# A hybrid decoder layer on one core: the MLP's two matrix products by seven block products for eight

## The chip, the core and the metric

The kernel runs on 1 core of a Trainium2 chip. The time is device microseconds of one launch: the median of 3 runs before the change is 2604.46 us (2600.12 to 2609.98). Engines are named as in the profile: PE (TensorE's matmuls), PEld (its weight loads), DVE (VectorE), ACT (ScalarE), POOL (GpSimd), SP (SyncE, which here only issues DMAs).

## The reference

One inference step of one decoder layer, for 512 prompt tokens and 8 short sequences of 4 tokens, 544 tokens in all, with a model width of 2048 and an MLP width of 8192, in float32:

```python
h = rmsnorm(x, norm_mix_w)
x = x + concat(conv_group(h), delta_group(h)) @ w_out
x = x + square(relu(rmsnorm(x, norm_ffn_w) @ w_up)) @ w_down
y = rmsnorm(x, final_norm_w)
```

Beside y it returns the new states of the convolution and delta groups. The change touches the second and the third line; the lines on the two head groups stay as they are.

## The kernel before

Activations lie transposed, channels on the 128 partitions and tokens along the free axis, in two token halves of 272 (256 prompt and 16 sample tokens). A matmul takes a 128x128 piece of a weight tile and 272 tokens of an activation tile into a PSUM bank.

Every product in float32 is made of three in float32r: `product` (lines 133 to 138) multiplies w_hi by x_hi, w_hi by x_lo and w_lo by x_hi, where hi is the value rounded and lo is the rest. A weight tile comes by one DMA into one of two w_raw buffers, ACT copies it into one of three w_hi buffers (line 112), and DVE subtracts that from w_raw into one of three w_lo buffers (line 115); `ahead` has two more tiles in work than the one that PE uses. These steps have a higher priority than the rest of the program, from which a scheduler makes one fixed order per engine; each engine and each DMA queue then runs its own in turn and waits on semaphores.

The stages, in time:

- The mixer (input projection, convolution, delta rule), to about 850 us. The change leaves it as it is.
- The output projection: 16 output tiles over the first 12 of 16 contraction tiles (w_o1, 32 loads of 128x768), then over the last 4 (w_o2, 8 loads of 128x1024, 48 matmuls each). A sum of 544 tokens goes from PSUM onto the residual x2 on DVE (line 876, `add`). Under w_o2, x2 times the norm's weight is split into h2's x_hi and x_lo (lines 127 and 130), ACT squares x2 (line 899), and POOL sums the squares in ssq (line 903). The token factor r2 = 1 / sqrt(mean + eps) isn't in h2: it is taken into the relu later.
- The MLP in 8 chunks of 1024 hidden channels. Up: 16 loads of 48 matmuls; for each of 8 hidden tiles DVE makes max(ps, 0) * r2 into f_tmp (line 920), ACT squares it (921) and copies u_hi (924), DVE makes u_lo (925). Down: 16 loads of 48 matmuls, each followed by `add` (876). u of a chunk and x2 stay in SBUF.
- The last chunk's down by token halves, 32 loads of 24 matmuls, with squares (ACT, line 949) summed on POOL (951 and 953) and the final norm of the first half, rstd (`rstd_rows`, lines 140 to 153) and DVE's scaling (line 939), under the products of the second. The second half's norm and its stores end the program.

Of the kernel before, what the change touches and what calls it, by code (L numbers as in the profile page):

```python
# [50 lines left out]
def trunk(ctx, tc, a):  # L51
# [119 lines left out]
    with ExitStack() as mix:  # L171
# [268 lines left out]
        def b_slab(ps, i):  # L440
            """Gate, then the group's RMSNorm as a side task."""
# [38 lines left out]
        # ---- gated delta rule of two heads  # L480
        def delta(gi, kq, vT, og):
# [8 lines left out]
            # keys with tokens on partitions, their norms, and the scalars that follow from them  # L490
# [21 lines left out]
            # decayed Gram matrices: at[m, 0, c] the system, at[m, 1, c] the output weights  # L512
# [19 lines left out]
            # inverse of the unit triangular systems: 32 x 32 blocks by substitution  # L532
# [36 lines left out]
            # values with tokens on partitions  # L569
# [11 lines left out]
            # blocks of 64, then of 128  # L581
# [39 lines left out]
            # the scan over chunks  # L621
# [40 lines left out]
            # RMSNorm over the value channels, and the gate  # L662
# [23 lines left out]
        def delta_sample(gi, kqs, vsT, og):  # L686
            """The 8 short sequences of two heads; rows are (k, q of head 0, k, q of head 1)."""
# [66 lines left out]
            # S += k y^T of each sequence in one pass: the float32r parts stacked along the contraction  # L754
# [38 lines left out]
        # ---- the input projection, with the other work threaded between its products  # L793
# [74 lines left out]
    ssq = tile_in(fp, "ssq2", [P, 2, HT])  # L868
    r2 = tile_in(fp, "r2", [P, 2, HT])

    def f_tmp():
        return tile_in(fp, "f_tmp", [P, 2, HT], bufs=4)

    def add(ob, ps, h=slice(0, 2)):
        with urgent():
            V.tensor_tensor(x2[ob][:, h], x2[ob][:, h], ps, ADD)  # L876
# [213 lines left out]
```

## Time and profile before

| | |
|---|---|
| median of 3 runs | 2604.46 us (2600.12 to 2609.98) |
| span of the profiled execution | 2602.0 us |
| PE busy | 2567.2 us, 99% |
| DVE, ACT, POOL busy | 1187.2, 776.5, 303.4 us |
| output projection w_o2, by PE | from 995 to 1043.5 us |
| MLP but its last down chunk, by PE | from 1043.5 to 2487.3 us |
| last down chunk, by PE | from 2487.3 to 2587 us |
| HBM traffic over the span | 101 GB/s |

All times of stages are microseconds from the start of the profiled span. A page of the profile has busy time by engine, the span in slices, the chain of waits that ended last (followed back from the last instruction), and groups of like instructions; the trace behind it gives single instructions with start and length. A matmul's record is longer than the distance to the next one, since matmuls overlap; a stage's price of one is its length over their number.

### The profile page before, as it was taken

What the parts mean: (1) busy time and instruction counts of PE and PEld (TensorE: products, weight loads), DVE (VectorE), ACT (ScalarE), POOL (GpSimd) and SP (SyncE); (2) the same over time, 40 slices, a digit from 0 to 9 for tenths busy, and PEclk for the clock granted to TensorE, in tenths of its full rate; (3) what the DMA queues carried; (4) which work ended last, traced back from release to release, by engine and by line L of the source; (5) the groups of instructions that cost most, each with busy time, mean ns of one, the idle gap of its engine ahead of it and who ended that gap; (6) DMA issues with size and microseconds to landing.
All of it is one profiled execution on the core that took longest, in us unless ns stands there. A gap on an engine that the chain in (4) does not pass through costs nothing.

```text
span 2602.0 us, 47137 instructions
## 1 busy us (share of the span) xinstructions
PE 2567.2 (99%) x20453; PEld 2545.1 (98%) x20453; DVE 1187.2 (46%) x1919; ACT 776.5 (30%) x1107; POOL 303.4 (12%) x413
## 2 busy tenths in 40 slices
PE   8999999999999999999999999999999999999997
PEld 8999999999999999999999999999999999999997
DVE  8675575675576325333333333333333333333346
ACT  5425325324234214321221221221221221221243
POOL 4224124123214003000000000000000000000022
PEclk9999999998999999999999999999999999999999
DMA  6333333343334522222222222222233222222245
GB/s 190 94 99 128 92 102 118 87 117 103 90 102 128 187 89 90 90 90 88 85 89 90 89 83 89 90 90 83 88 90 90 89 83 89 90 89 83 89 146 175
DMA packets 99256, 264.76 MB, mean 102 GB/s; under 512 B 28228, under 2 KB 35048, under 8 KB 99048
## 3 DMA queue, kind: packets, MB, share of 16 engines
q1 hardware_dynamic: 94824, 252.16, 31.8%
q0 software_dynamic: 4224, 9.59, 1.1%
q8 instruction: 161, 2.64, 0.4%
q14 instruction: 47, 0.39, 0.1%
HBM read 246.59 MB, written 15.10 MB: 101 GB/s over the span
## 4 chain that ended last, share of the span: by engine, by line
PE 89%; DVE 6%; DMA 2%; ACT 1%; issue 1%; SPq 0%; POOL 0%; DVEq 0%; ACTq 0%
PE ps_big L138 83%; DVE w_lo L115 2%; PE ps_sm L138 2%; DMA w_raw<-in_w_down_dram 1%; DVE xm L553 1%; DVE tm L549 1%; DMA tn<-ti 1%; ACT w_hi L112 0%; DVE x L939 0%; PE ps_sm L524 0%; DMA ti<-xm 0%; PE ps_sm L730 0%; PE ps_sm L636 0%; PE ps_sm L270 0%; DVE x_lo L130 0%
## 5 line engine op out<-in xcount | busy, mean ns | idle before, releaser
L138 PE MATMUL ps_big<-x_hi,w_hi 128*128 128x272 f32 x4320 | 906.3, 290 | 1.2 <-ACT x_hi L127 0.9
L138 PE MATMUL ps_big<-x_lo,w_hi 128*128 128x272 f32 x4320 | 903.7, 290 | 1.1 <-DVE x_lo L124 0.8
L138 PE MATMUL ps_big<-x_hi,w_lo 128*128 128x272 f32 x4320 | 901.0, 289 | 2.6 <-DVE w_lo L115 2.6
L112 ACT ACTIVATE w_hi<-w_raw 128x1024 fp32r<-128x1024 f32 (+2 forms) x427 | 442.9, 1037 | 1515.3 <-PE ps_big L138 1414.9
L115 DVE TENSOR_TENSOR w_lo<-w_raw,w_hi 128x1024 fp32r<-128x1024 f32 (+2 forms) x427 | 540.7, 1266 | 420.9 <-ACT w_hi L112 393.0
L138 PEld LDWEIGHTS ps_big<-x_hi,w_hi 128*128 128x128 f32 x4320 | 682.1, 189 | 5.8 <-ACT x_hi L127 2.1
L138 PEld LDWEIGHTS ps_big<-x_hi,w_lo 128*128 128x128 f32 x4320 | 682.1, 189 | 3.9 <-DVE w_lo L115 3.3
L138 PEld LDWEIGHTS ps_big<-x_lo,w_hi 128*128 128x128 f32 x4320 | 678.9, 189 | 1.9 <-DVE x_lo L124 1.0
L138 PE MATMUL ps_big<-u_lo,w_hi 128*128 128x272 f32 x1792 | 373.0, 289 | 0.0
L138 PE MATMUL ps_big<-u_hi,w_lo 128*128 128x272 f32 x1792 | 370.9, 288 | 0.0
L138 PE MATMUL ps_big<-u_hi,w_hi 128*128 128x272 f32 x1792 | 370.8, 288 | 0.0
L876 DVE TENSOR_TENSOR x<-x,ps_big 128x544 f32<-128x544 f32 x144 | 103.9, 722 | 492.2 <-PE ps_big L138 492.2
L138 PEld LDWEIGHTS ps_big<-u_hi,w_lo 128*128 128x128 f32 x1792 | 281.8, 188 | 0.0
L138 PEld LDWEIGHTS ps_big<-u_hi,w_hi 128*128 128x128 f32 x1792 | 281.5, 188 | 0.0
L138 PEld LDWEIGHTS ps_big<-u_lo,w_hi 128*128 128x128 f32 x1792 | 280.8, 189 | 0.0
L951 POOL COPY ssq<-f_tmp 128x272 f32<-128x272 f32 x2 | 2.3, 1148 | 1461.9 <-ACT f_tmp L949 1461.9
L920 DVE SCALAR_TENSOR_TENSOR f_tmp<-ps_big,r 128x544 f32<-128x544 f32 x64 | 46.4, 725 | 252.0 <-PE ps_big L138 252.0
L138 PE MATMUL ps_sm<-u_hi,w_lo 128*128 128x272 f32 x256 | 73.8, 289 | 1.4 <-DVE w_lo L115 1.4
L138 PE MATMUL ps_sm<-u_hi,w_hi 128*128 128x272 f32 x256 | 73.6, 288 | 0.2 <-ACT w_hi L112 0.2
L138 PE MATMUL ps_sm<-u_lo,w_hi 128*128 128x272 f32 x256 | 73.6, 288 | 0.0
L387 DVE SCALAR_TENSOR_TENSOR tmp<-tmp,cw 128x568 f32<-128x568 f32 (+1 forms) x88 | 70.9, 809 | 2.7
L366 DVE TENSOR_TENSOR tmp<-ps_big,r 128x512 f32<-128x512 f32 x47 | 32.4, 688 | 74.8 <-PE ps_big L138 74.7
(297 smaller groups left out, 1620.5 us busy)
## 6 DMA issues: line engine op xcount, KB each, us to landing
w_raw<-in_w_down_dram SPq DMA_DIRECT2D x144, 512.0 KB, 3.5
w_raw<-in_w_up_dram SPq DMA_DIRECT2D x128, 512.0 KB, 3.5
w_raw<-in_w_in_dram SPq DMA_DIRECT2D x106, 512.0 KB, 3.6
w_raw<-in_w_o_dram SPq DMA_DIRECT2D x32, 384.0 KB, 3.2
s<-in_s_d_dram SPq DMA_DIRECT2D x16, 512.0 KB, 3.6
tmp<-cat SPq DMA_DIRECT2D x16, 272.0 KB, 4.1
x<-in_x_dram SPq DMA_DIRECT2D x8, 544.0 KB, 6.1
out_o_y_dram<-x SPq DMA_DIRECT2D x16, 272.0 KB, 2.5
```

Source lines behind the costliest of these rows:

```text
L112: S.activation(hi[:, c], raw[:, c], AF.Copy)
L115: V.tensor_tensor(lo[:, c], raw[:, c], hi[:, c].bitcast(F32), SUB)
L138: PE.matmul(ps[h], wp[:, c : c + P], xp[:, h, :], start=start and i == 0, stop=stop and i == 2)
L366: V.tensor_tensor(out_p.rearrange("p (a c) -> p a c", a=2), whole[:, :, :HP], r1[:, :, :HP], MUL)
L387: V.scalar_tensor_tensor(co[:, :n], buf[:, i : i + n], cw[:, wcol + i : wcol + i + 1], co[:, :n], MUL, ADD)
L549: V.tensor_tensor(t, xm[:, :, j : j + 1].broadcast_to([P, 8, n]), um[:, j : j + 1, j + 1 :].broadcast_to([P, 8, n]), MUL,)
L553: V.tensor_tensor(xm[:, :, j + 1 :], xm[:, :, j + 1 :], t, SUB)
L876: V.tensor_tensor(x2[ob][:, h], x2[ob][:, h], ps, ADD)
L920: V.scalar_tensor_tensor(t, ps[1], 0.0, r2, MAX, MUL)
L951: G.tensor_copy(ssq[:, h, :], sq[:, h, :])
```

## The change

w_up, w_down and the activations are seen as 2x2 blocks: a pair of output tiles, a pair of contraction tiles, and the two token halves. Seven products of combined blocks stand for eight, in Winograd's form of Strassen's algorithm. Each is made of three float32r matmuls a piece, as before.

- `Weights` loads four tiles (a11, a12, a21, a22; w_q, of the new pool g with 10 buffers) for a pair m. At product 6 DVE makes four combinations of them, three in place; for each of the seven products ACT copies w_hi and DVE makes w_lo.
- `combos_first` and `combos` make the activation's blocks: c0 (two blocks as they are), c1 and c2 (two combinations each) and c3 (one block), each as hi and lo. The four combinations go into a tile tc of the pool tt, which has two buffers and holds u, ui, ssq and rt as well. c0 and c1 lie in the 32 buffers hl, c2 and c3 in the 24 of the new pool cmb.
- `bilinear` runs the products in the order 1, 2, 6, 5, 7, 3, 4, pair by pair; the last two pairs of a sequence are interleaved. Up has 32 pairs of hidden tiles (8 contraction pairs, 24 matmuls a product). Down has 5 chunks of 6 contraction pairs, 8 pairs of output tiles each (18 matmuls a product); the last 4 of 64 contraction tiles are multiplied in the ordinary way by token halves (w_d2, 32 loads of 128x512).
- u of a pair is stored to DRAM (u_d) by POOL's queue, and loaded again by `prepare`, which combines it on POOL. A chunk's tiles are prepared during the chunk before it: the first after pair 1, the second after pair 3, the rest after pair 5. Residual sums x2 lie in DRAM (x2_d): a pair's tile is loaded, added to seven times, and stored.
- w_o2 goes by token halves (16 loads of 24 matmuls), and the whole norm, r2 included, is applied to x2 ahead of the split (`normalise`): the first half's under the products of the second, the second half's behind rstd_rows at the end, with `combos` on DVE.

The core of the diff:

```diff
+    cmb = pool("cmb", 24)
+    gp = pool("g", 10)
+    tt = pool("tt", 2)
+    sqp = pool("sq", 2)
...
+    x2_d = [tile_in(dram, f"x2d{i}", [P, 2, 2, HT]) for i in range(KT // 2)]
+    u_d = [tile_in(dram, f"ud{i}", [P, 2, 2, HT]) for i in range(FF // 256)]
...
+    def f32r_parts(pl, name, tag, src):
+        hi = tile_in(pl, name + "_hi", [P, 2, HT], F32R, tag=tag)
+        lo = tile_in(pl, name + "_lo", [P, 2, HT], F32R, tag=tag)
+        S.activation(hi, src, AF.Copy)
+        V.tensor_tensor(lo, src, hi.bitcast(F32), SUB)
+        return hi, lo
+    def combos_first(c, b11_b21):
+        hi, lo = f32r_parts(hlp, "c0", "hl", b11_b21)
+        c[1], c[2] = (hi[:, 0, :], lo[:, 0, :]), (hi[:, 1, :], lo[:, 1, :])
+    def combos(c, x, eng):
+        b11, b12, b21, b22 = (x[:, i, j, :] for i in range(2) for j in range(2))
+        t = t_tile("tc")
+        eng.tensor_tensor(t[:, 1, :], b12, b11, SUB)
+        eng.tensor_tensor(t[:, 0, :], b22, t[:, 1, :], SUB)
+        eng.tensor_tensor(t[:, 2, :], b22, b12, SUB)
+        eng.tensor_tensor(t[:, 3, :], b21, t[:, 0, :], SUB)
+        hi, lo = f32r_parts(hlp, "c1", "hl", t[:, 0:2, :])
+        c[6], c[5] = (hi[:, 0, :], lo[:, 0, :]), (hi[:, 1, :], lo[:, 1, :])
+        b = tile_in(cmb, "c3", [P, 2, HT], F32R, tag="c")
+        S.activation(b[:, 0, :], b22, AF.Copy)
+        V.tensor_tensor(b[:, 1, :], b22, b[:, 0, :].bitcast(F32), SUB)
+        c[3] = b[:, 0, :], b[:, 1, :]
+        hi, lo = f32r_parts(cmb, "c2", "c", t[:, 2:4, :])
+        c[7], c[4] = (hi[:, 0, :], lo[:, 0, :]), (hi[:, 1, :], lo[:, 1, :])
+    ORDER = (1, 2, 6, 5, 7, 3, 4)
...
+                    self.q = [g_tile("w_q", [P, self.n]) for _ in range(4)]
+                    for t, s in zip(self.q, self.src):
+                        nc.sync.dma_start(t, s)
...
+                if p == 6:
+                    self.s1 = tile_in(rawp, "w_s1", [P, 1024], tag="w_raw")[:, : self.n]
+                    V.tensor_tensor(self.s1, a21, a22, ADD)
+                    V.tensor_tensor(a21, a11, a21, SUB)
+                    V.tensor_tensor(a11, self.s1, a11, SUB)
+                    V.tensor_tensor(a12, a12, a11, SUB)
+                s = {1: a11, 2: a12, 6: a11, 5: getattr(self, "s1", None), 7: a21, 3: a12, 4: a22}[p]
+                hi = tile_in(whip, "w_hi", [P, 1024], F32R)[:, : self.n]
+                lo = tile_in(wlop, "w_lo", [P, 1024], F32R)[:, : self.n]
+                S.activation(hi, s, AF.Copy)
+                V.tensor_tensor(lo, s, hi.bitcast(F32), SUB)
+            return hi, lo
...
+            if p == 6:
+                at = flat.index(w)
+                for nxt in flat[at + 1 : at + 2]:
+                    nxt.load()
+            return w.parts(p)
...
+            ps = st[{2: "y", 5: "z", 3: "z"}.get(p, "x")]
+            c = cs(key)
+            for k, ck in enumerate(c):
+                xhi, xlo = ck[p]
+                for j, (wp, xp) in enumerate(((whi, xhi), (whi, xlo), (wlo, xhi))):
+                    PE.matmul(
+                        ps, wp[:, k * P : (k + 1) * P], xp,
+                        start=p in (1, 2, 5) and k == j == 0, stop=k == len(c) - 1 and j == 2,
+                        skip_group_check=True,
+                    )
+            st["out"](p, ps)
...
-    for oq, w in ahead(range(KT * N2 // 8), lambda q: weight(a["w_o2"][q], 1024)):
+    steps = [(h, q) for h in range(2) for q in range(KT * N2 // 8)]
+    for (h, oq), w in ahead(steps, lambda it: weight(a["w_o2"][it[1]], 1024)):
...
+        nc.gpsimd.dma_start(x2_d[oq][:, :, h, :], x2p[oq][:, :, h, :])
+        if h == 1:
+            if oq == 1:
+                rstd_rows(r2, [ssq], t_tile("rt", (P, 2, HT)), (0,))
+            if oq >= 2:
+                for i in {2: (0, 1), 7: (6, 7)}.get(oq, (oq - 1,)):
+                    normalise(i, 0)
+                    combos_first(h_c[i], x2p[i][:, :, 0, :])
+    with urgent():
+        rstd_rows(r2, [ssq], t_tile("rt", (P, 2, HT)), (1,))
+        for i in range(KT // 2):
+            normalise(i, 1)
+            combos(h_c[i], x2p[i], V)
...
+    def hidden(m):
+        t = t_tile("u").rearrange("p (a b) c -> p a b c", a=2)
+        def out(p, ps):
+            with urgent():
+                if p in (1, 6, 5, 4):
+                    d = {1: t[:, 0, 0], 6: t[:, 0, 1], 5: t[:, 1, 1], 4: t[:, 1, 0]}[p]
+                    S.activation(d, ps, AF.Copy)
+                else:
+                    add({2: t[:, 0, 0], 7: t[:, 1, 1], 3: t[:, 0, 1]}[p], ps)
+                if p in (3, 4):
+                    d = t[:, 0 if p == 3 else 1]
+                    V.scalar_tensor_tensor(d, d, 0.0, d, MAX, MUL)
+                    if p == 4:
+                        nc.gpsimd.dma_start(u_d[m], t)
...
+        return [[x] for x in w[:-2]] + [w[-2:]]
+    bilinear(pairs_of(NF, lambda m, q: a["w_up"][m, q], 1024), lambda m: h_c, hidden)
+    CH = 6
+    NCH = (NF - 2) // CH
+    u_c = {}
+    def load_u(k):
+        x = t_tile("ui").rearrange("p (a b) c -> p a b c", a=2)
+        nc.sync.dma_start(x, u_d[k])
+        return x
+    def prepare(k):
+        x, u_c[k] = load_u(k), [None] * 8
+        combos_first(u_c[k], x[:, :, 0, :])
+        combos(u_c[k], x, G)
+    def partial(key):
+        c, m = key
+        x = g_tile("x2v", [P, 2, 2, HT])
+        nc.sync.dma_start(x, x2_d[m])
+        def out(p, ps):
+            for b, h in {1: [(0, 0)], 2: [(0, 0)], 6: [(0, 1)], 5: [(1, 1)], 7: [(1, 1)], 3: [(0, 1)], 4: [(1, 0)]}[p]:
+                add(x[:, b, h], ps)
+            if p == 4:
+                nc.gpsimd.dma_start(x2_d[m], x)
+                if c + 1 < NCH and m in (1, 3):
+                    prepare(CH * (c + 1) + m // 2)
+                if c + 1 < NCH and m == KT // 2 - 3:
+                    for k in range(2, CH):
+                        prepare(CH * (c + 1) + k)
...
+    for k in range(CH):
+        prepare(k)
...
+    bilinear(groups, lambda key: [u_c[CH * key[0] + k] for k in range(CH)], partial)
+    u = []
+    for k in range(NCH * CH, NF):
+        x = load_u(k)
+        for b in range(2):
+            u.append(f32r_parts(hlp, "ul", "hl", x[:, b]))
...
-    for (h, ob), w in ahead(steps, lambda it: weight(a["w_down"][(NCH - 1) * KT + it[1]], 1024)):
+    for (h, ob), w in ahead(steps, lambda it: weight(a["w_d2"][it[1]], 512)):
```

Three places of the order that the scheduler makes of it. On DVE at the start of up, before: the last weight splits of the output projection, rstd (r_10067), and the first hidden tiles.

```order
L115 TENSOR_TENSOR w_lo<-w_raw,w_hi 128x1024
L150 TENSOR_TENSOR f_tmp<-r_10067 128x272 x2
L151 SCALAR_TENSOR_TENSOR f_tmp<-ps_sm,f_tmp 128x272 x2
L152 TENSOR_SCALAR f_tmp<-f_tmp 128x272 x2
L153 TENSOR_TENSOR r_10067<-r_10067,f_tmp 128x272 x2
L920 SCALAR_TENSOR_TENSOR f_tmp<-ps_big,r_10067 128x544
L115 TENSOR_TENSOR w_lo<-w_raw,w_hi 128x1024
L925 TENSOR_TENSOR u_lo<-f_tmp,u_hi 128x544
L115 TENSOR_TENSOR w_lo<-w_raw,w_hi 128x1024
```

The same engine and place now: the last step of rstd (r_88), the first pair's norm (L1008), its combinations tc (L920 to L923, now the lines of `combos`), splits of c3 (L928) and c2 (L909), and the next pair.

```order
L154 TENSOR_TENSOR r_88<-r_88,rt 128x272
L1008 SCALAR_TENSOR_TENSOR x_7_10063<-x_7_10063,nv,r_88 128x272
L1008 SCALAR_TENSOR_TENSOR x_0_10056<-x_0_10056,nv,r_88 128x272 x2
L920 TENSOR_TENSOR tc<-x_0_10056 128x272
L922 TENSOR_TENSOR tc<-x_0_10056 128x272
L921 TENSOR_TENSOR tc<-x_0_10056,tc 128x272
L928 TENSOR_TENSOR c_12226<-x_0_10056,c_12226 128x272
L923 TENSOR_TENSOR tc<-x_0_10056,tc 128x272
L1008 SCALAR_TENSOR_TENSOR x_1_10057<-x_1_10057,nv,r_88 128x272 x2
L909 TENSOR_TENSOR c_lo<-tc,c_hi 128x544
L920 TENSOR_TENSOR tc<-x_1_10057 128x272
```

Before, the splits of weights go on at once; now the norm and the combinations of the eight pairs stand between rstd and the sixth product's activations.

On SP at the change from up to down, now: the last loads for up, two quartets for down (the first of x2v and half a third quartet with them), and the loads of u for the first chunk.

```order
L946 DMA w_q<-in_w_up_dram 128x1024 x126
L946 DMA w_q<-in_w_d_dram 128x768 x8
L1084 DMA x2v<-x2d_10072 128x1088
L946 DMA w_q<-in_w_d_dram 128x768 x2
L1073 DMA ui<-ud_10080 128x1088
L1073 DMA ui<-ud_10081 128x1088
L1073 DMA ui<-ud_10082 128x1088
L1073 DMA ui<-ud_10083 128x1088
```

On POOL's queue beside it: the stores of the last two u tiles, then the combinations of the first u tile and the start of the second's.

```order
L1056 DMA ud_10110<-u 128x1088
L1056 DMA ud_10111<-u 128x1088
L920 TENSOR_TENSOR tc<-ui 128x272
L922 TENSOR_TENSOR tc<-ui 128x272
L921 TENSOR_TENSOR tc<-ui,tc 128x272
L923 TENSOR_TENSOR tc<-ui,tc 128x272
L920 TENSOR_TENSOR tc<-ui 128x272
```

Before, SP had only loads of w_raw there, and POOL had nothing between the second norm and the last chunk; now each load of ui and each tc follows the stores of u in its queue, and they share the two buffers of tt.

On DVE in down, before: a weight's split and a sum of 544 tokens for each 48 matmuls (an output tile).

```order
L876 TENSOR_TENSOR x_0_10050<-x_0_10050,ps_big 128x544
L115 TENSOR_TENSOR w_lo<-w_raw,w_hi 128x1024
L876 TENSOR_TENSOR x_1_10051<-x_1_10051,ps_big 128x544
L115 TENSOR_TENSOR w_lo<-w_raw,w_hi 128x1024
L876 TENSOR_TENSOR x_1_10051<-x_1_10051,ps_big 128x544
```

Now, the start of a pair m in the middle of a chunk: the weights' combinations (L953 to L956), splits (L961), and sums of 272 tokens onto x2v.

```order
L953 TENSOR_TENSOR w_s_21785<-w_q 128x768
L961 TENSOR_TENSOR w_lo<-w_q,w_hi 128x768
L954 TENSOR_TENSOR w_q<-w_q 128x768
L883 TENSOR_TENSOR x2v<-x2v,ps_s 128x272
L961 TENSOR_TENSOR w_lo<-w_q,w_hi 128x768
L955 TENSOR_TENSOR w_q<-w_s_21605,w_q 128x768
L883 TENSOR_TENSOR x2v<-x2v,ps_s 128x272
L956 TENSOR_TENSOR w_q<-w_q 128x768
L961 TENSOR_TENSOR w_lo<-w_q,w_hi 128x768
L883 TENSOR_TENSOR x2v<-x2v,ps_s 128x272
L961 TENSOR_TENSOR w_lo<-w_s_21605,w_hi 128x768
L883 TENSOR_TENSOR x2v<-x2v,ps_s 128x272
```

Each sum waits for the PE product it belongs to, and the weight work of the next products stands behind it in the same queue.

More of the change, by code (lines that the diff above doesn't have):

```diff
@@ L886, in trunk, with bank @@
         if q == 1:
-            add(ob, ps[1])
-    h2 = []
-    N2 = KT - N1
-    for oq, w in ahead(range(KT * N2 // 8), lambda q: weight(a["w_o2"][q], 1024)):
+            add(x2[ob], ps[1])
+    early.close()
+    small2 = pool("small2", 4, space=PSUM)
+    def bank(first):
+        t = tile_in(small2 if first else small, "ps_s", [P, 512], tag="sm2" if first else "sm")
+        return t[:, :HT]
+    def f32r_parts(pl, name, tag, src):
[4 more added lines that the diff above has]
+        return hi, lo
@@ new lines, in bilinear, with load @@
+    def bilinear(groups, cs, outs):
+        items = [(g, i, p) for g in range(len(groups)) for p in ORDER for i in range(len(groups[g]))]
+        flat = [w for g in groups for w, _ in g]
+        def load(it):
+            g, i, p = it
+            w = groups[g][i][0]
+            w.load()
+            if p == 6:
[3 more added lines that the diff above has]
+            return w.parts(p)
+        state = {}
+        for (g, i, p), (whi, wlo) in ahead(items, load):
+            w, key = groups[g][i]
+            if p == 1:
+                state[i] = {"x": bank(True), "out": outs(key)}
+            st = state[i]
+            if p in (2, 5):
+                st["y" if p == 2 else "z"] = bank(False)
+            ps = st[{2: "y", 5: "z", 3: "z"}.get(p, "x")]
[9 more added lines that the diff above has]
+            st["out"](p, ps)
@@ L894, in trunk @@
             for k in range(N2):
[L895 to L899 removed]
+                product({h: ps}, w, (N2 * j + k) * P, cat[N1 + k], k == 0, k == N2 - 1, (h,))
+            add(x2[ob][:, h], ps)
+            sq = tile_in(sqp, "sq", [P, HT])
+            S.activation(sq, x2[ob][:, h], AF.Square)
@@ new lines, in trunk @@
+    xt = [[None] * (KT // 2) for _ in range(2)]
+    def finish(h, pair):
+        t = xt[h][pair]
+        for j in range(2):
+            o = 2 * pair + j
+            V.scalar_tensor_tensor(t[:, j], t[:, j], nv[:, 32 + o : 33 + o], r3[:, h, :], MUL, MUL)
+        nc.sync.dma_start(a["o_y"][pair][:, :, h, :], t)
+    steps = [(h, o) for h in range(2) for o in range(KT)]
+    for (h, ob), w in ahead(steps, lambda it: weight(a["w_d2"][it[1]], 512)):
+        pair, j = divmod(ob, 2)
+        if j == 0:
+            xt[h][pair] = tile_in(cmb, "xt", [P, 2, HT], tag="c")
+            nc.sync.dma_start(xt[h][pair], x2_d[pair][:, :, h, :])
+        x = xt[h][pair][:, j]
+        ps = ps_small(HT)
+        for k in range(4):
+            product({h: ps}, w, k * P, u[k], k == 0, k == 3, (h,))
+        add(x, ps)
+        sq = tile_in(sqp, "sq", [P, HT])
+        S.activation(sq, x, AF.Square)
+        if ob == 0:
+            G.tensor_copy(ssq[:, h, :], sq)
+        else:
+            (G if ob < KT - 2 else V).tensor_tensor(ssq[:, h, :], ssq[:, h, :], sq, ADD)
```

112 lines of the change are left out of this document (48 added, 64 removed).

## The prediction

> **What bounds the kernel now.** I read the page first, then the busy time by stage, then the chain of waits, then single groups and DMA sizes. The first row is the page's line on TensorE.
>
> ```profile
> PE 2567.2 (99%) x20453; PEld 2545.1 (98%) x20453; DVE 1187.2 (46%) x1919; ACT 776.5 (30%) x1107; POOL 303.4 (12%) x413
> ```
>
> By stage (length, busy time of PE, PEld, DVE, ACT, POOL, granted clock, DMA share, GB/s): the second output projection, the MLP, its last down chunk, the end, and two stretches of the mixer.
>
> ```profile
> 980.00:1043.00 63.00, 63.00 (x500) 63.00 (x500) 39.62 (x45) 32.73 (x44) 24.24 (x16) 1.00 0.29 88
> 1043.00:2487.00 1444.00, 1444.00 (x11480) 1443.84 (x11479) 467.72 (x485) 334.74 (x369) 0.00 (x0) 1.00 0.29 88
> 2487.00:2587.00 100.00, 98.42 (x777) 97.13 (x775) 62.54 (x88) 44.67 (x65) 36.98 (x26) 1.00 0.57 170
> 2587.00:2602.00 15.00, 1.10 (x4) 0.30 (x2) 8.68 (x21) 1.35 (x3) 0.00 (x0) 0.61 0.43 149
> 700.00:750.00 50.00, 50.00 (x405) 49.85 (x403) 31.72 (x77) 17.57 (x50) 6.20 (x15) 1.00 0.31 91
> 750.00:800.00 50.00, 48.27 (x416) 46.75 (x415) 37.29 (x93) 10.49 (x12) 10.89 (x18) 0.95 0.37 107
> ```
>
> In the MLP PE never waits and every other engine is under a third busy: there a matmul less is its whole time less. The chain of waits (start, length) gives the price of one.
>
> ```profile
> 1044.43 1442.91 PE ps_big L138 x11472
> 2487.34 24.02 PE ps_sm L138 x191
> 2513.78 3.90 DMA w_raw<-in_w_down_dram
> ```
>
> 1442.91 / 11472 = 0.1258 us for each matmul. The last chunk, 32 loads for 24 matmuls each, takes 2487.3 to 2587, 3.12 us a load against 24 x 0.1258 = 3.02: two raw buffers only just feed it.
>
> **The change part by part.** The span is 2602.0 us, 2.5 below the median of 2604.46; I sum spans and add 2.5 at the end. Up to the last w_o1 tile nothing of weight moves.
>
> What it removes: the MLP had 8 x 32 x 48 = 12288 matmuls. Now up has 32 pairs x 7 products x 24 = 5376, the five down chunks 40 x 7 x 18 = 5040, the ordinary rest 32 x 12 = 384: 10800, so 1488 fewer, 187 us at 0.1258. Everything else is what this buys, and the question is how much of it PE then spends waiting.
>
> Prices on VectorE, from starts in its timeline (start, duration): what counts in a full queue is the distance of starts.
>
> ```profile
> 40.33 0.95 DVE L115 TENSOR_TENSOR w_lo<-w_raw,w_hi 128x768 fp32r<-128x768 f32 x1
> 41.19 0.72 DVE L239 TENSOR_TENSOR ssq<-ssq,tmp 128x544 f32<-128x544 f32 x1
> 41.83 0.41 DVE L253 TENSOR_TENSOR wst<-wab,wst 128x256 fp32r<-128x256 f32 x1
> 42.16 1.22 DVE L115 TENSOR_TENSOR w_lo<-w_raw,w_hi 128x1024 fp32r<-128x1024 f32 x1
> ```
>
> So 768 wide costs 0.86, 544 costs 0.64, 256 costs 0.33 (272: 0.35), and 1024 by the same slope 1.15. The end of the program, in the same view, prices the norm.
>
> ```profile
> 2586.93 0.44 DVE L876 TENSOR_TENSOR x<-x,ps_sm 128x272 f32<-128x272 f32 x1 [0.33 <-PE ps_sm L138]
> ...
> 2591.45 6.69 DVE L939 SCALAR_TENSOR_TENSOR x<-x,nv,r 128x272 f32<-128x272 f32 x16
> ```
>
> *w_o2 by halves.* 16 loads at 3.12 instead of 384 matmuls, 48.3 us: +1.7. Under its second half VectorE also gets the norm of the first and four-wide splits: per load 1.15 + 2 x 0.35 + 2 x 0.42 + 0.64 = 3.3 us, against 3.02, and more while POOL adds squares: early in the run, with POOL in a long add, the 768 split that takes 0.95 took twice that.
>
> ```profile
> 11.92 1.99 DVE L115 TENSOR_TENSOR w_lo<-w_raw,w_hi 128x768 fp32r<-128x768 f32 x1
> ```
>
> Six such loads: 2 to 8 us, I take 3. The MLP starts at 1043.5 + 4.7 = 1048.2. [...]
>
> *Start of up.* From the last add to the end of rstd was 4.5 us (2586.93 to 2591.45). Now there is a POOL add in it (1.4, below), three norm steps and one split between its VectorE steps (1.9) and some backlog: 9 us. Then product 6 of the first pair needs the combinations of all eight pairs, and VectorE's order has in front of the last one 16 norm steps (6.7), 32 combinations of 272 (11.2), 7 splits of 272 (2.5), 16 of 544 (10.2), 7 instructions of 1024 (8.1), one add, and about 1.5 us where one combination waits for another: 40.5 us. PE has 3 products to do in it, 72 x 0.1258 = 9.06. Wait: 9 + 40.5 + 0.5 - 9 = 41 us (36 to 46). Before, the MLP began without a gap, since its norm was put into f_tmp behind the products.
>
> *Up.* 5376 x 0.1258 = 676.3. Per pair VectorE has 11 x 1.15 + 3 x 0.35 + 2 x 0.75 = 15.2 us in 21.1, its bursts reach about 5.7 us at product 6 against two products of 3.02 of lead: covered, barely.
>
> *Up to down.* Sizes and landing times of DMAs, and POOL's groups (mean ns):
>
> ```profile
> x<-in_x_dram SPq DMA_DIRECT2D x8, 544.0 KB, 6.1
> out_o_y_dram<-x SPq DMA_DIRECT2D x16, 272.0 KB, 2.5
> out_o_ss_dram<-s POOLq DMA_DIRECT2D x8, 512.0 KB, 3.8
> w_raw<-in_w_o_dram SPq DMA_DIRECT2D x8, 512.0 KB, 3.5
> xr<-in_x_dram SPq DMA_DIRECT2D x7, 544.0 KB, 4.5
> ...
> cat<-tmp POOLq DMA_DIRECT2D x8, 256.0 KB, 2.8
> cat<-o_g POOLq DMA_DIRECT2D x8, 256.0 KB, 3.6
> ```
>
> ```profile
> L953 POOL TENSOR_TENSOR ssq<-ssq,f_tmp 128x272 f32<-128x272 f32 x24 | 34.7, 1445 | 43.5 <-ACT f_tmp L949 43.5
> ...
> L471 POOL DMA_DIRECT2D cat<-tmp x16 | 11.3, 735 | 37.3 <-DVE xm L553 32.9 <-DVE tmp L469 4.4
> ...
> L432 POOL TENSOR_TENSOR tmp<-tmp 128x512 f32<-128x512 f32 x8 | 10.3, 1283 | 23.6 <-DVE tmp L366 23.6
> ```
>
> The pool tt has two buffers, and both hold u of the last two pairs until their stores land. Then u is read back, one tile in one buffer and its combinations in the other, so the six preparations are serial: a load of 544 KB (4.5, bounds 3.5 and 6.1) and four POOL combinations (0.68 each by proportion from the 512-wide row, 1.45 by the 272 row; I take 0.9, since most of VectorE stands still then). Period 8.1 us. The first tile: last u but one done 3 us before the end, a copy and a square 1.2 us, 0.7 to issue, 3.8 to store, 4.5 to load: it lands about 8 us after up ends, the sixth at 8 + 5 x 8.1 = 48.5. Products 1, 2 and 6 need tile 6, so the wait is 48 us (38 at 3.5 and 0.68; 67 at 6.1 and 1.45).
>
> *Down.* 5040 x 0.1258 = 634.0. VectorE 11 x 0.86 + 7 x 0.35 = 11.9 us of 15.85 a pair, plus 2.3 for a preparation; weights, residual tiles and stores are 2.7 MB in 15.85 us, 170 GB/s, what the last chunk moves now, and the u tiles come on top. I put 6 us for small waits (0 to 30).
>
> *Four chunk boundaries.* 24 of 32 hl buffers and 18 of 24 cmb buffers are the running chunk's, so tiles 1 and 2 of the next are ready, the third is half written, and three of them are loaded and combined in series after it: tile 4 lands 1.5 us after the chunk's last product, tile 6 two periods later at 17.7: 17 us each, 68 together (48 to 100).
>
> *After a wait.* PE's clock falls when it idles: 0.95 over 50 us above, that is 5 us at half speed or 2.5 us lost, in a stretch with under 2 us of idling. At half clock two matmuls start 0.45 us apart, 0.225 each:
>
> ```profile
> 592.00:600.00 8.00, 8.00 (x56) 7.20 (x54) 4.97 (x18) 1.46 (x3) 1.03 (x1) 0.50 0.00 0
> ```
>
> ```profile
> 594.27 0.66 PE L138 MATMUL ps_big<-x_hi,w_hi 128*128 128x272 f32 x2
> 594.72 0.66 PE L138 MATMUL ps_big<-x_lo,w_hi 128*128 128x272 f32 x2
> ```
>
> Six waits at 2.5: 15 us. [...] But the row shows 8 us of work without a gap at half clock; what would follow from that is a rival below.
>
> *The rest.* ScalarE's copies of 850 to 1043 us by shape:
>
> ```profile
> L112 ACT ACTIVATE w_hi<-w_raw 128x768 fp32r<-128x768 f32 x28 | 23.7, 845 | 94.6 <-PE ps_big L138 94.6
> ...
> L112 ACT ACTIVATE w_hi<-w_raw 128x1024 fp32r<-128x1024 f32 x11 | 11.6, 1058 | 16.5 <-PE ps_big L138 14.9 <-ACT f_tmp L899 1.5
> ```
>
> 32 loads of 256 KB pass through two buffers, each held for the load (3.2, between 2.8 and 3.6), the copy (0.63 at 512 wide by these two) and VectorE's split (0.95 and 1.22 above give 0.68): 4.5 / 2 = 2.25 us a load, 72 us (64 to 80) for 48.3 of matmuls. The end, as now, 15 (2587 to 2602).
>
> Sum: 1048.2 + 41 + 676.3 + 48 + 640 + 68 + 15 + 72 + 15 = 2623.5, with 2.5 more 2626: 187 us are saved and some 209 given back, slower by 0.8%. A measurement of this kernel can tell about 0.5%, 13 us, from no change: 2591.4 to 2617.5 is the same.
>
> **The rivals.**
>
> *Short waits (faster).* The serial steps run at their lower bounds: loads of 3.5, combinations of 0.68. Then 1046 + 36 + 676.3 + 38 + 634 + 48 + 6 + 64 + 15 = 2563, 2566 as a median. For it: the 512 KB row, and that nothing else moves data while PE waits. Against: the two 544 KB rows, 4.5 and 6.1, and that c_hi and c_lo read the same tile while POOL does. A microsecond of the period is worth 5 + 4 x 2 = 13; with the small terms (after a wait, the rest, down's waits) at their lower ends too, 23 us, it decides from a period of 7.2 down: 23 + 0.9 x 13 = 35, which is 2591.
>
> *VectorE bounds down (slower still).* At product 6 four weight combinations and a split, 5 x 0.86 = 4.3 us and a ScalarE copy between, stand ahead of the PSUM adds; PE's lead is two products, 4.5 us. If each pair loses 1.5 us, 40 pairs lose 60: 2686. For it: 75% busy with adds that wait for PE in the same queue. Against: three weight buffers, and the order spreads the four over three products. It decides where VectorE passes 90% of a pair.
>
> *PE stays at half clock around every wait.* The last stage feeds PE 1.5 us of work in 2.25; at 0.225 a matmul a step is 2.7, 32 of them 86 instead of 72; and three products after each wait (6.8 us, up 9) at half speed cost 7 us instead of 2.5, six times 27: 2626 + 14 + 27 = 2667. For it: the row at 592. Against: 2487 to 2587 shows 1.00 with PE at 98%. [...]
>
> **How the numbers follow.** The forecast gets 0.42, with its own range from 2600 to 2655; short waits 0.30, VectorE 0.13, half clock 0.15. Faster by over 0.5%: short waits and a little of the forecast's lower end, 0.32. The same: 0.20, from the forecast. Slower: 0.48. The range runs from the first rival's 2566 to 2690, past the second's; half of short waits and part of VectorE lie outside.
>
> **What would show it.** PE's idle time before its first products: some 41 us near 1050 behind VectorE's splits, 48 near 1770 behind ui loads and POOL, four of 17 some 127 us of matmuls apart, each behind ui. Matmuls in up and down at 0.126. If the boundaries show under 12 us, or the ui period under 7.2, the first rival holds; if PE waits in every pair of down for VectorE, the second; if the granted clock after 2500 is under 0.8, the third. If PE's count isn't 1488 lower or its pace differs, all of it is wrong.

## The result and the profile after

The changed kernel takes 2650.55 us (median of 4 runs, 2645.77 to 2654.69) where the kernel before takes 2607.22 (4 runs, 2600.12 to 2611.01): a ratio of 1.0172, 95% interval 1.0148 to 1.0196. It is slower, as forecast, and inside the range, but by 1.7% instead of 0.8%: the loss is twice the one that the prediction worked out. The profiled execution has a span of 2652.8 us, against a predicted sum of 2623.5: 29 us are to be explained.

The page's line of busy time first. PE runs 1492 matmuls fewer (1488 by count; some records are missing) and 128 us less; VectorE has 673 us more to do, POOL 167.

```profile
PE 2439.2 (92%) x18961; PEld 2389.9 (90%) x18961; DVE 1860.5 (70%) x2899; ACT 1028.7 (39%) x1542; POOL 470.9 (18%) x639
```

By stage, as in the prediction (length, busy time of PE, PEld, DVE, ACT, POOL, granted clock, DMA share, GB/s): the start of up, up, the change to down with most of chunk 0's first products, the boundary to chunk 1, the steady part of chunk 1, and the w_d2 stage.

```profile
1041.00:1099.00 58.00, 25.88 (x101) 19.93 (x99) 55.12 (x107) 26.51 (x44) 5.80 (x7) 0.62 0.30 102
1099.00:1758.00 659.00, 658.28 (x5269) 658.28 (x5270) 496.96 (x505) 269.29 (x347) 15.99 (x30) 1.00 0.37 125
1758.00:1850.00 92.00, 48.66 (x301) 44.27 (x299) 54.56 (x75) 31.70 (x50) 37.07 (x40) 0.70 0.36 119
...
1942.00:2006.00 64.00, 42.77 (x293) 39.97 (x293) 48.57 (x63) 24.04 (x37) 28.85 (x27) 0.81 0.45 154
2006.00:2096.00 90.00, 90.00 (x721) 90.00 (x721) 73.96 (x107) 35.43 (x44) 2.97 (x6) 1.00 0.53 169
...
2557.00:2637.00 80.00, 61.12 (x385) 52.40 (x383) 45.79 (x87) 34.26 (x67) 22.75 (x29) 0.96 0.55 170
```

Two rows read 1.00 and full PE: up and the steady part of a chunk run at the old pace (721 matmuls in 90 us, 0.125 each) with VectorE at 75% and 82%. What is lost lies outside them, and in the rows at 1758 and 1942 POOL is busy 40% and 45% of the time, against 2% and 3% in the two full ones. The list of PE's waits over the whole run says for what (total us, times, longest):

```profile
PE ps_s L992 <- ACT c_hi L908: 94.5, 20, 10.4
PE ps_s L992 <- DVE c_lo L909: 37.6, 14, 16.8
PE ps_s L992 <- DVE x2v L883: 17.3, 12, 2.1
```

c_hi and c_lo are the prepared activations (hi and lo of c0 to c2), 132 us of waiting, 102 of it in down; in down, weights come to 7.5 us. The chain of waits through one preparation between up and down (start, length):

```profile
1773.33 3.48 DMA ui<-ud
1776.94 0.76 POOL tc L920
1777.70 1.21 POOL tc L922
1778.91 0.93 POOL tc L921
1779.91 0.77 POOL tc L923
1780.70 3.65 DMA ui<-ud
```

Load, four combinations on POOL, next load: the period is 7.4 us, strictly in series, as the prediction had it (8.1). The chain's long PE pieces give the price of a chunk: the same run of 665 matmuls starts in chunks 0 to 3 at

```profile
1850.13 85.10 PE ps_s L992 x665
2005.49 83.52 PE ps_s L992 x665
2159.82 83.66 PE ps_s L992 x665
2315.45 83.59 PE ps_s L992 x665
```

that is about 155 us apart, where a chunk has 1008 matmuls, 126.8 us. Measured at the last matmul ahead of each boundary (1944.62, then 2408.60 three chunks later) it is 154.7: each chunk loses 27.9 us.

### The profile page after: what moved, and what is told of

The parts are those of the page before. It is cut to its first block, busy times and chain, and to the rows that moved or that the text cites. A ratio compares the mean times of both kernels' runs of the same rounds, so it can differ in the third digit from the quotient of the medians.

```text
span 2652.8 us, 46768 instructions
## 1 busy us (share of the span) xinstructions
PE 2439.2 (92%) x18961; PEld 2389.9 (90%) x18961; DVE 1860.5 (70%) x2899; ACT 1028.7 (39%) x1542; POOL 470.9 (18%) x639
## 4 chain that ended last, share of the span: by engine, by line
PE 73%; DVE 11%; DMA 7%; POOL 3%; issue 3%; ACT 3%; SPq 1%; DVEq 0%; ACTq 0%; POOLq 0%
PE ps_s L992 42%; PE ps_big L139 25%; DMA ui<-ud 3%; DVE w_lo L116 2%; PE ps_sm L139 2%; DVE w_lo L961 2%; DMA w_raw<-in_w_d_dram 1%; POOL tc L921 1%; DVE c_lo L909 1%; DVE xm L554 1%; POOL tc L922 1%; DMA w_q<-in_w_d_dram 1%; DMA x2d<-x2v 1%; DVE tm L550 1%; POOL tc L920 1%
## 5 line engine op out<-in xcount | busy, mean ns | idle before, releaser
L992 PE MATMUL ps_s<-c_hi,w_hi 128*128 128x272 f32 x2976 | 869.6, 294 | 121.1 <-ACT c_hi L908 94.5
L992 PE MATMUL ps_s<-c_lo,w_hi 128*128 128x272 f32 x2976 | 872.9, 293 | 37.6 <-DVE c_lo L909 37.6
L992 PE MATMUL ps_s<-c_hi,w_lo 128*128 128x272 f32 x2976 | 869.1, 292 | 0.7 <-DVE w_lo L961 0.7
L992 PEld LDWEIGHTS ps_s<-c_hi,w_hi 128*128 128x128 f32 x2976 | 570.3, 192 | 132.2 <-ACT c_hi L908 100.4
L992 PEld LDWEIGHTS ps_s<-c_lo,w_hi 128*128 128x128 f32 x2976 | 572.9, 193 | 45.3 <-DVE c_lo L909 45.2
L992 PEld LDWEIGHTS ps_s<-c_hi,w_lo 128*128 128x128 f32 x2976 | 573.8, 193 | 1.3 <-DVE w_lo L961 1.3
L961 DVE TENSOR_TENSOR w_lo<-w_q,w_hi 128x768 fp32r<-128x768 f32 (+1 forms) x432 | 471.2, 1091 | 124.9 <-ACT w_hi L960 122.2
L139 PE MATMUL ps_big<-x_hi,w_hi 128*128 128x272 f32 x2144 | 456.9, 293 | 1.2 <-ACT x_hi L128 0.9
L139 PE MATMUL ps_big<-x_hi,w_lo 128*128 128x272 f32 x2144 | 452.9, 292 | 2.6 <-DVE w_lo L116 2.6
L139 PE MATMUL ps_big<-x_lo,w_hi 128*128 128x272 f32 x2144 | 452.8, 292 | 1.1 <-DVE x_lo L125 0.8
L1090 POOL DMA_DIRECT2D x2d<-x2v x40 | 21.9, 547 | 479.6 <-DVE x2v L883 477.9
```

Of the source, the lines that this page charges most:

```text
L139: PE.matmul(ps[h], wp[:, c : c + P], xp[:, h, :], start=start and i == 0, stop=stop and i == 2)
L961: V.tensor_tensor(lo, s, hi.bitcast(F32), SUB)
L992: PE.matmul(ps, wp[:, k * P : (k + 1) * P], xp, start=p in (1, 2, 5) and k == j == 0, stop=k == len(c) - 1 and j == 2, skip_group_check=True,)
```

## The experiments

Theories. **S**: PE waits for preparations in series, since two tt buffers hold one tile's load and combination; the size of the loss is their period and their number. **D**: VectorE's queue is the bound in down. **C**: POOL's combinations slow VectorE's instructions while they run, so their price isn't only their own time. Beside these, the half clock after a wait (behind the one between up and down, from 1811.59 to 1816.97, the granted clock is 0.50 and matmuls start 0.227 us apart), and SP's queue, in which loads of u stand behind weight loads that wait.

The runs are compared from a common mark, since the mixer, which no edit touches, ends anywhere from 843 to 854 us: from the first matmul of the long w_o1 piece of the chain (`PE ps_big x1094`, at 849.64 in the changed kernel) to the end of the span. Each row is one execution; how much this stretch varies between executions of one kernel wasn't measured, so a difference of one or two us says nothing.

| kernel | span, us | mark to end, us |
|---|---|---|
| before | 2602.0 | 1752.0 |
| changed | 2652.8 | 1803.2 |
| combinations of u on VectorE | 2592.9 | 1749.4 |
| loads of u by POOL's queue | 2661.0 | 1811.3 |
| dummy matmuls in the waits | 2651.1 | 1804.5 |
| table loaded ahead of the norm | 2643.6 | 1796.1 |
| start of up shared with POOL | 2651.4 | 1804.1 |
| VectorE's, plus idle POOL work beside | 2626.3 | 1773.6 |
| three tt buffers alone | 2622.1 | 1774.1 |
| VectorE's + table | 2585.0 | 1739.4 |
| the same + three tt buffers | 2573.3 | 1719.7 |
| the same + w_d2 through nine buffers | 2549.3 | 1697.5 |

### The combinations of u on VectorE

```diff
-        combos(u_c[k], x, G)
+        combos(u_c[k], x, V)
```

> In `prepare` the four combinations of a u tile are made on VectorE instead of POOL, nothing else. Theory S (what the down phase loses, it loses to the serial chain of ui load and combinations through tt's two buffers): a period of 7.45 us holds 3.6 us of POOL work, on VectorE four starts 0.35 to 0.48 apart, 1.6; so the period falls to about 5.4, the wait between up and down from 52 to about 42 us, a chunk boundary loses 4 us less twice over two periods, and the slow first two pairs of a chunk (POOL and VectorE in each other's way, some 3 us each) are gone: span 2652.8 down to 2605 to 2630. Rival D (VectorE is what bounds down): 1.6 us more per tile on it makes each chunk 5 to 10 us longer, span 2660 or more.

Measured: 1749.4 from the mark, 53.8 us less, more than S alone gave, and the opposite of D. VectorE runs 120 instructions more, some 42 us at 0.35, and yet is busy only 6.8 us longer (1867.3 for 1860.5): its other instructions have become shorter. The chain through one preparation now:

```profile
1771.95 3.55 DMA ui<-ud
...
1775.59 0.44 DVE tc L920
1776.03 0.35 DVE tc L922
1776.38 0.64 DVE c_lo L909
1777.02 0.35 DVE tc L921
1777.37 0.35 DVE c L928
1777.72 0.36 DVE tc L923
1778.15 3.59 DMA ui<-ud
```

The period falls from 7.4 to 6.2: POOL's four took 3.7 in series; VectorE's four take 1.5, with 1.0 of splits that it does between them anyway. Chunk 0 gains 14.9 us, each of the next three some 10.6 (a chunk 144.0 instead of 154.7). At the first boundary PE's gaps ahead of product 6 give 5.2 of this (17.6 us before, 1.64 + 6.45 + 4.36 = 12.45 now); the rest, about half, is gained at half clock and in the pairs behind it, where PE awaits no preparation. D falls as the bound of a whole chunk; S explains the first part, not the second.

### POOL busy beside VectorE, with nothing waiting for it

The kernel above, and POOL makes four subtractions of 272 for each u tile into scratch that nobody reads. Nothing else is changed.

```diff
         combos(u_c[k], x, V)
+        if not shadow:
+            for i in range(2):
+                shadow.append(tile_in(sqp, "sq", [P, HT]))
+                G.memset(shadow[i], 0.0)
+        for i in range(4):
+            G.tensor_tensor(shadow[i % 2], u_c[k][1 + i // 2][1].bitcast(F32), shadow[i % 2], SUB)
```

> As e1 (combinations on VectorE), but POOL also makes four subtractions of the same size for each u tile, from c0's lo into a scratch tile that nobody waits for; they can't lengthen the chain of ui. Theory C: what e1 gained is in good part that POOL no longer runs beside VectorE: of its 50 us in down, 20 to 35 come back, span 2613 to 2628. Theory S alone (POOL's time in the chain): within 6 us of e1's 2592.9.

Measured: 1773.6, 24.2 us back of the 53.8. The chain in the same place:

```profile
1781.11 0.35 DVE tc L922
1781.47 0.64 DVE c_lo L909
1782.10 0.35 DVE tc L921
1782.45 0.92 DVE c L928
1783.38 0.93 DVE tc L923
1784.37 3.56 DMA ui<-ud
```

The first three cost what they cost without POOL. Then POOL starts, and the last two, 0.35 and 0.36 alone, take 0.92 and 0.93. The groups of like instructions over down say the same (busy us, mean ns), first with POOL idle there, then with the scratch work:

```profile
L909 DVE TENSOR_TENSOR c_lo<-tc,c_hi 128x544 fp32r<-128x544 f32 x60 | 42.6, 721 | 0.3
L961 DVE TENSOR_TENSOR w_lo<-w_s,w_hi 128x768 fp32r<-128x768 f32 x40 | 38.1, 953 | 0.6 <-ACT w_hi L960 0.6
```

```profile
L909 DVE TENSOR_TENSOR c_lo<-tc,c_hi 128x544 fp32r<-128x544 f32 x60 | 57.6, 983 | 0.3
L961 DVE TENSOR_TENSOR w_lo<-w_s,w_hi 128x768 fp32r<-128x768 f32 x38 | 42.2, 1111 | 0.0
```

So work on POOL that nobody waits for costs time: C is shown. It isn't POOL's queue that is held up: 35 of the 40 stores of x2v behind the scratch work still find POOL idle, waiting for VectorE's sums. It isn't the same instructions that are slowed in the changed kernel, so 24 us is the size of the effect and not an exact share. There, the group of c and one of the weight combinations read, over the same window,

```profile
L954 DVE TENSOR_TENSOR w_q<-w_q 128x768 f32<-128x768 f32 x36 | 38.8, 1078 | 0.0
...
L928 DVE TENSOR_TENSOR c<-ui,c 128x272 fp32r<-128x272 f32 x30 | 21.5, 718 | 0.0
```

against 952 and 434 ns with POOL idle. It goes both ways: a POOL combination takes 0.76 us with VectorE idle (from 1950.08 to 1955.94), and about 1.5 beside VectorE's work, by POOL's timeline in the changed kernel,

```profile
1955.39 0.76 POOL L920 TENSOR_TENSOR tc<-ui 128x272 f32<-128x272 f32 x1 [8.01 <-DMA ui<-ud]
...
1979.40 1.51 POOL L920 TENSOR_TENSOR tc<-ui 128x272 f32<-128x272 f32 x1 [3.94 <-DVE x2v L883]
```

and in VectorE's timeline beside it a 768-wide instruction takes 0.95, and the next one 1.53:

```profile
1979.33 0.95 DVE L961 TENSOR_TENSOR w_lo<-w_q,w_hi 128x768 fp32r<-128x768 f32 x1
1980.19 1.53 DVE L953 TENSOR_TENSOR w_s<-w_q 128x768 f32<-128x768 f32 x1
```

### The start of up shared with POOL

```diff
-            combos(h_c[i], x2p[i], V)
+            combos(h_c[i], x2p[i], G if i in (2, 4, 6) else V)
```

> At the start of up the combinations of three of the eight pairs (2, 4, 6) go to POOL, the other five stay on VectorE; nothing else. My first working (VectorE's 40 us of work are what PE waits for): 12 combinations of 0.35 less, 4 us less: span 2648. Theory C (POOL and VectorE slow each other when both read SBUF: that is the term the forecast missed): POOL's combinations of 0.8 to 1.5 stretch the splits beside them and stand themselves in the chain of pairs; no gain or a loss, span 2652 to 2665.

Measured: 1804.1, 0.9 more. Twelve of the 32 combinations leave the queue that PE waits for, and nothing is gained. POOL's combinations there take 0.77 to 1.76 us, and VectorE's timeline has a 1024-wide split before them (1.22) and one beside them (1.80). C fits; how much of the missing gain is C and how much the waits between the two queues, this run doesn't tell.

```profile
1068.09 1.22 DVE L961 TENSOR_TENSOR w_lo<-w_q,w_hi 128x1024 fp32r<-128x1024 f32 x1
1072.88 1.80 DVE L961 TENSOR_TENSOR w_lo<-w_s,w_hi 128x1024 fp32r<-128x1024 f32 x1
```

### Three tt buffers

```diff
-    gp = pool("g", 10)
+    gp = pool("g", 9)
-    tt = pool("tt", 2)
+    tt = pool("tt", 3)
```

> The changed kernel with a third buffer in tt and nine instead of ten in g; the combinations stay on POOL. Counted from the same matmul of w_o1 to the end the changed kernel took 1803.2 us, e7 1739.4 and e8, e7 with the third buffer, 1719.7. Theory S and C apart: a load runs under POOL's combinations, so the period between up and down falls from 7.45 to about 4, 17 us there, and 2 to 4 us at each of four boundaries; POOL still stretches VectorE's work in the first pairs: 1803 down to 1772 to 1782. If only POOL beside VectorE mattered: 1795 or more.

Measured: 1774.1, 29.1 us less than the changed kernel, with the combinations still on POOL. PE's waits for c_hi between up and down fall from about 5.4 us to 1.7 to 2.4 each:

```profile
1772.32 0.82 PE L992 MATMUL ps_s<-c_hi,w_hi 128*128 128x272 f32 x2 [2.35 <-ACT c_hi L908]
1777.10 0.82 PE L992 MATMUL ps_s<-c_hi,w_hi 128*128 128x272 f32 x2 [1.72 <-ACT c_hi L908]
```

This is S shown by itself: a load beside a combination, and the period of PE's waits is 4.8 us.

### The loads of u by POOL's queue

```diff
-        nc.sync.dma_start(x, u_d[k])
+        nc.gpsimd.dma_start(x, u_d[k])
```

> The loads of u (ui) are issued from POOL's queue instead of SP's, nothing else. Theory S with the queue: at a chunk boundary the fifth ui stands on SP behind two weight loads, one of which waits for the store of the chunk's last residual tile to land (ui issued at 1951.4, its buffer free at 1947.4). On POOL's queue it starts when its buffer is free: 4 us less at each of four boundaries, and the weight loads no longer stand behind ui: 16 to 28 us, span 2625 to 2637. Rival (the buffers and the load itself set it, not the queue): within 6 us of 2652.8. Against both, POOL's issue of some 0.6 us and stores now queued behind ui could add up to 10 us.

Measured: 1811.3, 8.1 us more. At the boundaries a load of u does stand on SP behind weight loads that wait. Out of that queue PE's gap for it falls (from 6.7 to 8.0 us to 4.5 to 5.8), but PE's wait in the second pair behind grows (from 1.2 to 2.1 us to 3.6 to 4.0), and the period between up and down grows to 8.05 (loads at 1772.14 and 1780.17, 0.3 us more to issue and 0.3 more to land). Over the whole, SP's queue isn't what costs the time.

### Dummy matmuls in the waits

Forty matmuls into a bank that is never read stand ahead of each late tile's first product, so that PE works while it waits.

```diff
             for k, ck in enumerate(c):
+                if p == 1 and isinstance(key, tuple) and key[1] == 0 and k >= (3 if key[0] else 1):
+                    dm = bank(False)
+                    for _ in range(40):
+                        PE.matmul(dm, whi[:, :P], c[0][1][0], start=True, stop=True, skip_group_check=True)
```

> Ahead of each late contraction tile of the first product of a chunk (tiles 4 to 6, in the first chunk 2 to 6), 40 matmuls of data that are there already are made into a PSUM bank that nobody reads, so that PE has some 5 us of work in each gap. Rival H (the loss that the forecast missed is PE's half clock behind each wait): the granted clock stays near 1.00 through the boundary, the last tile's matmuls and product 6 run at 0.126 instead of 0.23, and each of the five places is 2.5 to 4 us shorter, 12 to 20 in all: span 2633 to 2641. Theory S: the arrival of ui sets the end of the boundary, and only the work behind the last arrival gains: 0 to 8 us, or a loss where the extra matmuls are still running when a tile arrives.

Measured: 1804.5, 1.3 us more, although the mean granted clock rises from 0.950 to 0.974 and PE's waits from 1755 to 1860 us shrink from 43.6 us in sum to 23.4. From the mark, the long run of chunk 0 starts 2.6 us later than in the changed kernel (1003.1 and 1000.5):

```profile
1849.67 83.58 PE ps_s L996 x665
```

Behind the last late tile PE, now at full clock (0.126 us from matmul to matmul in products 6 and 5), waits 3.0 us for a sum on VectorE at a place where at half clock (0.227 in product 6) it didn't wait:

```profile
1817.80 0.48 PE L996 MATMUL ps_s<-c_hi,w_hi 128*128 128x272 f32 x1 [3.04 <-DVE x2v L883]
```

In this run a slow clock is a sign of waiting, not its price: what the faster PE gains it waits away. The dummy matmuls may have a price of their own (product 6 starts 1.4 us later from the mark), which this run doesn't separate.

### The activation table ahead of the norm

In the kernel before, one load ahead of the norms (1.28 us, at 1040.35) gives ScalarE a table that serves both of rstd's functions; from there to the end there is no other. The change dropped that call, in a line that the core of the diff above leaves out, and rstd now loads a table at each of its two lines, four times each. The first pair is at 1022.99 and 1024.79; the view of the run from 1030 us on has the other three:

```profile
L149 ACT ACT_TABLE_LOAD x3 | 3.8, 1283 | 0.1
L150 ACT ACT_TABLE_LOAD x3 | 3.8, 1283 | 0.1
```

```diff
+                ln_exp(True)
                 rstd_rows(r2, [ssq], t_tile("rt", (P, 2, HT)), (0,))
```

> The table that holds both Ln and Exp is loaded ahead of the second norm, as before the change; without it ScalarE loads a table of 1.28 us ahead of Ln and another ahead of Exp in each rstd. At the start of up and at the end of the program these stand on the path: theory: 2.5 us less at each, 5 us in all, span 2646 to 2649. Rival (they lie under other waits): no change, 2651 to 2655.

Measured: 1796.1, 7.1 us less. One load at 1020.44 stands for the eight. In the last rstd, on the chain, the two functions now follow each other with no load between:

```profile
2630.28 0.50 ACT r L149
...
2630.79 0.44 ACT r L150
```

### What adds up, and a version that beats both

The combinations on VectorE and the table together:

> e1 and e6 together: a u tile's combinations on VectorE, and the Ln and Exp table loaded ahead of the norms. e1 stood at 2592.9, e6 took 5 to 9 us off: 2584 to 2588 if they add up, since they lie in other stages.

Measured: 1739.4, 63.8 less: 53.8 and 7.1 add up, within 3 us. Then with three tt buffers (and nine of g):

> As e7, with a third buffer in tt, paid for by one of the ten buffers of g. Theory S (two buffers make load and combinations serial): a load now runs under the combinations before it, the period of 6.2 us between up and down falls towards the load's 3.6 to 4.2, 5 x 2 = 10 us there and 4 to 5 at each of four boundaries: span 2556 to 2568. Rival: g is what down lives on; with nine buffers weights or residual tiles come later, each of 40 pairs loses some tenths of a us and up's start waits for its first quartet: 2580 to 2610.

Measured: 1719.7, another 19.7 less, where the expectation adds up to 26 to 30; PE's waits between up and down are 1.0 to 2.0 each. Last, the 32 loads of w_d2 go through g's nine buffers, which are free by then, instead of the two of w_raw:

```diff
+    def weight_g(src):
+        with urgent():
+            raw = g_tile("w_g", [P, 512])
+            hi = tile_in(whip, "w_hi", [P, 1024], F32R)[:, :512]
+            lo = tile_in(wlop, "w_lo", [P, 1024], F32R)[:, :512]
+            nc.sync.dma_start(raw, src)
+            S.activation(hi, raw, AF.Copy)
+            V.tensor_tensor(lo, raw, hi.bitcast(F32), SUB)
+        return hi, lo
...
-    for (h, ob), w in ahead(steps, lambda it: weight(a["w_d2"][it[1]], 512)):
+    for (h, ob), w in ahead(steps, lambda it: weight_g(a["w_d2"][it[1]])):
```

> e8, and the last 32 weight loads (w_d2) come into the buffers of g, nine of them, instead of the two of raw. The changed kernel has a load, a copy of 0.64 and a split of 0.70 in series twice over, 2.45 us for a tile of 1.51 us of matmuls, 78 us in that stage. With nine buffers PE sets it: 32 x 1.51 = 48 and a start of 2 to 4: 25 us less than e8 (1719.7 from the same matmul on), 1692 to 1698, a time of 2546 to 2556 and a ratio to the kernel before of 0.976 to 0.983. Rival: ScalarE and VectorE with squares, adds and the first half's norm set it: 10 us less than e8, 2565.

Measured: 1697.5, another 22.2 less. The first half of the stage is PE's own, 215 matmuls at 0.125:

```profile
2480.19 26.89 PE ps_sm L139 x215
```

This kernel takes 2547.38 us (median of 5 runs, 2541.62 to 2553.69) against 2605.98 for the kernel before on the same chip (9 runs): a ratio of 0.9773, interval 0.9747 to 0.98. The seven products are worth 2.3% once the preparations cost less; PE still waits 42.2 us for c_hi and 20.9 for c_lo in it.

## Why the prediction was half right

What was gained came as worked out: the count of matmuls and their pace. What was given back, term by term (predicted, then measured):

| term of the sum | predicted, us | measured, us | difference |
|---|---|---|---|
| start of the MLP | 1048.2 | 1041.2 | -7.0 |
| start of up, up, its half clock | 719.8 | 718.2 | -1.6 |
| wait between up and down | 48 | 47.7 | -0.3 |
| four chunk boundaries | 68 | 86.5 | +18.5 |
| half clock after down's five waits | 12.5 | 14.5 | +2.0 |
| small waits in down | 6 | 14.6 | +8.6 |
| w_d2 | 72 | 79.1 | +7.1 |
| end | 15 | 17.0 | +2.0 |

The differences sum to 29.3. A wait's measured loss is the stretch from the start of PE's last matmul ahead of it to the start of its product 6, less 0.1258 for each matmul in it: 1759.27 to 1811.59 with 37 matmuls between up and down, 1944.33 to 1967.70 with 17 at the first boundary (21.2; the others 21.6 to 21.9). What down loses beyond these is 29.1 us: PE stands idle for 14.6, and the rest goes to matmuls at half clock behind the late starts and some of these waits. The prediction has 2.5 us of half clock after each wait; half clock between one late tile and the next (granted clock 0.53 from 1759.60 to 1811.50, 0.57 from 1943.50 to 1967.65) is part of the wait here.

**Start of the MLP.** 1043.5 was no start of the MLP but only a break between two pieces of the chain: the row `850.02 193.49 PE ps_big L138 x1526` runs on into up. w_o1's 1094 and w_o2's 384 matmuls end at 850.02 + 1478 x 0.1258 = 1036, or some 1037 with the small gaps in it. The increment of w_o2 by halves was right (4 to 5 us for 4.7, of which 1.7 should have read 1.6); its base was 6 to 7 late. That this error and those of w_d2 and the end cancel is luck; it leaves down with the whole difference.

**The waits for preparations** were right in mechanism, and ahead of down in size too. Start of up: 41.9 us lost where 41 and 2.5 were put, two table loads that it didn't have among them. Between up and down the period is 7.4 for 8.1, with loads at 3.6 instead of 4.5 and POOL's four at 3.7, close to the 3.6 that were put.

**Down's boundaries and small waits** are the steps that failed. The first is "17 us each": the prediction let a wait end where tile 6 lands. At the boundaries it lands 18.4 to 19.0 us after the chunk's last product, where 17.7 was put, but POOL's combinations of that tile, their copy, their split and a sum on VectorE come behind it, and product 6 starts 4.9 us after the landing, at every one of the five late starts. Between up and down:

```profile
1803.14 3.57 DMA ui<-ud
...
1808.83 0.93 POOL tc L921
...
1811.59 4.24 PE ps_s L992 x17
```

There PE has 36 matmuls to do meanwhile, 4.5 us, which make up for it; at a boundary it has 16, 2.0 us, and loses 21.6 in the mean.

The second is "I put 6 us for small waits (0 to 30)": PE is idle for 14.6, inside that range. These waits, 0.6 to 2.1 us at a time, lie in the pairs just behind each late start, half for sums on VectorE (x2v) and half for weights (w_hi). VectorE has to catch up there, while POOL goes on with the next preparations: it is busy 91% of the time behind the first boundary, against 82% in the steady pairs.

```profile
1968.00:2006.00 38.00, 34.42 (x256) 33.41 (x256) 34.62 (x46) 16.06 (x24) 16.21 (x14) 0.96 0.47 164
```

Beside these stands a price that was put at nothing. The prediction had the row that says what POOL does to VectorE (the 768 split at 1.99 beside POOL's add) and applied it to w_o2 alone; for `prepare` it put POOL at 0.9 an instruction "since most of VectorE stands still", and VectorE at no extra cost. In the runs POOL's take 0.76 to 1.5 us, VectorE's take up to 1.53 for 0.95 at 768 wide and 0.92 for 0.35 at 272, and work on POOL that nothing waits for costs 24 us. VectorE's add from PSUM (x2v) shows no such price: its group has a mean of 433 ns with POOL idle and 431 with the scratch work, and in the changed kernel the adds at 1981.65 and 1984.56, beside POOL's combinations, take 0.42 and 0.43. What makes the others slow each other the runs don't show.

**w_d2 and the end.** The loads of 256 KB that stand on the chain mostly take 3.4 to 4.0 us where 3.2 was put (the median of all 32 is 2.7), and rstd loads two tables at 1.28 in each of the two stages: without the table loads the kernel was 7.1 faster over their four places.

**The rivals.** *Short waits* was to hold below a period of 7.2; it came to 7.4, and three buffers show what it would have been worth. *VectorE bounds down* falls as it was put, for every pair: in the steady pairs VectorE is at 82% and PE at 100%. In the pairs behind a late start, at 91%, it does hold PE up. *Half clock* falls by its own test: the clock of the w_d2 stage is 0.96 although PE is 76% busy there, and the dummy matmuls raised it elsewhere for nothing. What stays open is how the 29 us that down loses behind its late starts divide between VectorE's slowing by POOL and VectorE's backlog after a late start, which would be there without it: moving the combinations took POOL away and shortened the late start at once.

## What to carry to other kernels

The operation moved to an idle engine had two prices here: its own chain (four combinations in 3.7 us on POOL, 1.5 on VectorE), and what it does to an engine that works beside it (24.2 us for POOL work that nothing waits for); price both wherever the two run side by side. A wait for a prepared tile ended here not when its data landed but when the tile's own preparation was done, 4.9 us later. Where a tile needs a buffer for its load and another for its work, count the buffers: with two, load and work took turns here in a period of 7.4 us, and a third was worth 20 to 29 us. A gain of the bounding engine's work arrives only with its stages fed: here the same 1488 matmuls were worth -1.7% or +2.3%.

## What the hardware showed that was not expected

- Beside each other, POOL's and VectorE's instructions both took longer: 272 wide on POOL 0.76 us alone and about 1.5 beside VectorE in the changed kernel, 272 wide on VectorE 0.35 alone and 0.92 beside POOL's scratch work.
- A low granted clock cost nothing that the runs could show: from 0.950 to 0.974 in the mean with the time unchanged (1803.2 and 1804.5 from the mark), and PE at full clock (0.126 us a matmul) waited 3.0 us for VectorE where at half clock (0.227) it hadn't waited.
- In the changed kernel rstd's two functions each loaded a table of 1.28 us, eight loads in all; with one load in their place, which serves both, ScalarE was busy 8.9 us less (1019.8 for 1028.7) and the time was 7.1 us shorter.
